# Key layer of a two-block transformer: ten chunks of the first table loaded while the queries are formed, and 100 tokens instead of 96 handled by gathered rows

## The chip, the core and the metric

The kernel runs on one core of a Trainium2 chip. The core has five engines that work side by side: TensorE (PE) multiplies matrices and writes to PSUM, VectorE (DVE) and ScalarE (ACT) do elementwise work, GpSimd (POOL) here issues the indirect loads, and SyncE (SP) issues most of the ordinary loads. Sixteen DMA engines move the data. The metric is the time of one execution on the device in microseconds (us). The median of three runs of the kernel before is 1599.38 us (1598.18 to 1601.05).

## What is computed

Two transformer blocks, one after the other, on 256 tokens of width 1024. The change lies in the last stage of the second block, the key layer:

```python
def peer(h, wq, keys1, keys2, u_tab, v_tab):      # per chunk of 128 tokens, xc: 128 x 1024
    q = (xc @ wq).reshape(128, 8, 2, 128)
    s1 = einsum('chd,hnd->chn', q[:, :, 0], keys1);  v1, i1 = top_k(s1, 16)
    s2 = einsum('chd,hnd->chn', q[:, :, 1], keys2);  v2, i2 = top_k(s2, 16)
    # the 16 best of the 256 sums, for each of 8 heads; expert = i1 * 128 + i2
    best, pos = top_k(v1[..., :, None] + v2[..., None, :] ..., 16)
    g = softmax(best)
    a = einsum('chkd,cd->chk', u_tab[eidx], xc)
    return einsum('chk,chkd->cd', gelu(a) * g, v_tab[eidx])
```

There are 128 x 128 = 16384 experts, each with a row of 1024 numbers in the first table (`u_tab`) and one in the second (`v_tab`). Every token picks 8 x 16 = 128 of them.

## The kernel before

The key layer handles the tokens in two ways at once.

**Dense tokens.** For the last ND = 160 of the 256 tokens (their count is ND = 256 - NG) every expert is computed. The tables are cut into 128 chunks of 128 experts; a chunk of a table is one load of 512 KB. In the first pass, for each chunk c, eight matmuls (L1640) multiply the chunk of the first table by the 160 tokens, and ACT applies the GELU and puts the result into column c of `B` (128 x 128 x 160, the activations' matrix; `act`, L1601). From chunk C0 = 40 on, the routing weights are multiplied in, four tokens at a time (`gbuild`; its four matmuls are L1968). In the second pass, for each chunk, eight matmuls (L1648) multiply `B` by the chunk of the second table and add up in eight PSUM buffers. So there are 1024 matmuls in each pass, with 160 columns each.

**Gathered tokens.** For the first NG = 96 tokens only the picked rows are fetched. They come in NS = 3 sets of GN = 32 tokens; one indirect load (L1768, issued by POOL) fetches 128 rows of 8 KB, first and second table side by side. DVE multiplies and sums these rows up (L1796, L1782); 32 such loads make a set, whose sums come into the dense result by eight small matmuls (L1653). `gathers(n)` is called once per chunk and lets so many steps of `gathered` be written down that they make 9/20 of the chunks of the first pass and 7/20 of those of the second. Step j issues gather j+4 (the first issues five), and a gather waits for the last matmul of the chunk before (`pace_pe`).

**Order of the work.** Before the first pass stand the queries: for each m of 16, `col_tile` loads a tile of `wq`, ACT (L97) and DVE (L98) split it in two parts, PE multiplies (L132 to L138), and two matmuls (L1564) give the scores, which ACT copies into a part of `B` not yet used (L1565). DVE searches the best 16 (`routing`, L1835 to L1911), 128 tokens after the other 128; for the first half it ends in `picks`, where ACT issues the DMAs that lay out the picked numbers (`gi`) and weights (`gw`) for the gathers (L1753). Three transposes on PE (L1928) take over the results of each half; they wait for DVE (the cast of L1921). `expand` (L1730, L1734) copies the gathered tokens' inputs on POOL, transposes them on PE and leaves one tile `xd` for each set.

**Loads.** The chunks of the tables take turns in ten buffers (four `wA`, three `hi`, three `lo`), and SP issues the load of a chunk (L87) when PE is done with the chunk that had the buffer. A scheduler puts the instructions of each engine in a fixed order by a timeline of its own.

The functions that the change touches follow; the line numbers are those of the profile.

Of the kernel before, what the change touches and what calls it, by code (L numbers as in the profile page):

```python
# [19 lines left out]
D = 1024  # L20
# [24 lines left out]
class K:  # L45
# [21 lines left out]
    def wload(self, src, shape, eng=None):  # L67
        pools = self.wpools
        p, tag = pools[self.wi % len(pools)]
        self.wi += 1  # L70
        if p is None:

            v = tag[:, :math.prod(shape)]
            if len(shape) == 2:
                v = v.rearrange("p (a b) -> p a b", a=shape[0])
            (eng or self.nc.sync).dma_start(v, src)
            return v
        if self.wrap and self.wi == len(pools):
# [8 lines left out]
        (eng or self.nc.sync).dma_start(v, src)  # L87
        return v
# [1439 lines left out]
    C0 = 40  # L1528
    NS, GN = 3, 32
    GG = 128 // GN  # L1530
    GJ = 128 // GG
    NG = NS * GN
    ND = S - NG

# [8 lines left out]
    def peer(self):  # L1543
# [14 lines left out]
        rg = self.routing([Bf[:, 128 * ND - 8192 + 2048 * t:128 * ND - 6144 + 2048 * t] for t in range(2)], Sc)  # L1558
        late = None

# [10 lines left out]
        for m in range(16):  # L1571
# [34 lines left out]

        nj = self.NS * self.GJ

        def gathers(n):
# [41 lines left out]
        def summed(s, k):  # L1651

            nc.tensor.matmul(acc[k][:, s * self.GN:(s + 1) * self.GN], self.sums[s][:, k * 128:(k + 1) * 128], self.sel,  # L1653
                             start=False, stop=False)

# [66 lines left out]
    def expand(self, x32):  # L1722

        nc = self.nc
        n, G = self.GN, self.GG
        self.picked = False
        self.gx = [self.T(self.rt, [128, D], F32, "xd%d" % s) for s in range(self.NS)]
        for s in range(self.NS):
            w = self.T(self.gp, [128, 2 * D], F32, "g")[:, 0:D].rearrange("p (k g t) -> p k g t", k=8, g=G)
            nc.gpsimd.tensor_copy(w, x32[:, :, None, s * n:(s + 1) * n].to_broadcast([128, 8, G, n]))  # L1730
            for hf in range(2):
# [6 lines left out]
    def picks(self, e0, e1, w):  # L1738

        nc = self.nc  # L1740
        n, J = self.GN, self.GJ
        t = self.T(self.gp, [128, 2 * D], F32, "g")
        f, wc, idi = t[:, 0:128], t[:, 128:256], t[:, 256:384].bitcast(I32)
        self.gi = self.T(self.rt, [128, self.NS, J], I32, "gi")
        self.gw = self.T(self.rt, [128, self.NS, J], F32, "gw")
        self.ga = self.T(self.rt, [128, self.NS, J], F32, "ga")
# [3 lines left out]
        for s in range(self.NS):  # L1750
# [3 lines left out]
        self.sel = self.T(self.rt, [128, n], F32, "gsel")  # L1754
        nc.scalar.dma_start(self.sel, self.A["sel"])
        self.picked = True

    def gathered(self):

        nc, A = self.nc, self.A  # L1760
        stt = nc.vector.scalar_tensor_tensor
        J, n = self.GJ, self.NS * self.GJ
        buf, acc = {}, self.T(self.rt, [128, D], F32, "xa")

        def fetch(i):
            if i < n:
                buf[i] = self.xg[:, i % 5 - 3, :] if i % 5 > 2 else self.T(self.gp, [128, 2 * D], F32, "g")
                ins = nc.gpsimd.indirect_dma_start(  # L1768
                    out=buf[i], out_offset=None, in_=A["uv"],
                    in_offset=bass.IndirectOffsetOnAxis(ap=self.gi[:, i // J, i % J:i % J + 1], axis=0))  # L1770
                if self.pace_pe:
# [4 lines left out]
        def add(i):  # L1776
            nonlocal acc
            s, j = i // J, i % J
            t, a, w = buf.pop(i)[:, D:], self.ga[:, s, j:j + 1], self.gw[:, s, j:j + 1]
            nc.vector.tensor_tensor(w, w, a, op=OP.mult)  # L1780
# [12 lines left out]
        for i in range(n):  # L1793
            s, j = i // J, i % J
            t, a = buf[i][:, 0:D], self.ga[:, s, j:j + 1]
            stt(t, t, 1.0, self.gx[s], op0=OP.mult, op1=OP.mult, accum_out=a)  # L1796
# [243 lines left out]
def _prep(I):  # L2040
# [54 lines left out]
    for n in ("w_gate", "w_up", "w_down"):  # L2095
# [23 lines left out]
                                 P["v"].reshape(-1, D)], 1))  # L2119
    P["sel"] = np.tile(np.eye(K.GN, dtype=np.float32), (K.GG, 1))  # L2120
    P["fnorm"] = _f(I["final_norm_g_2"][None])
# [36 lines left out]
```

## Time and profile before

| | |
|---|---|
| median of three runs | 1599.38 us (1598.18 to 1601.05) |
| profiled execution, its time | 1600.43 us |
| its span, from the first to the last instruction | 1598.6 us |
| PE busy | 1521.2 us (95%) |
| DVE busy | 954.7 us (60%) |
| ACT busy | 496.1 us (31%) |
| POOL busy | 125.7 us (8%) |
| moved by DMA | 536.5 MB, on average 336 GB/s |
| first pass of the key layer (L1640) | 975.9 to 1299.5 us |
| second pass (L1648) | 1299.5 to 1584 us |

The profile takes one execution; its span lies 1.8 us below that execution's own time. A float32 matmul stands as two records of PE. Records of PE overlap, so their pitch (the time of a long row divided by its count) is what one costs, not the duration of one. PEclk is the TensorE clock that was granted: 1.00 is 2.4 GHz and 0.50 is 1.2 GHz.

### The profile page before, as it was taken

How to read it: one execution, taken by the hardware profiler on the slowest of the kernel's cores; microseconds unless marked ns; L12 is line 12 of the kernel's file. 1: busy time of each engine (PE TensorE's matmuls, PEld its weight loads, DVE VectorE, ACT ScalarE, POOL GpSimd, SP SyncE). 2: the span in 40 equal slices, each digit the busy share in tenths (PEclk: the TensorE clock that was granted, in tenths of full speed). 3: DMA queues.
4: the chain of work that ended last, by engine and by line, in shares of the span. 5: the costliest groups of instructions: out<-in, count | busy, mean ns of one | idle time of the engine just before them, and what ended most of it. 6: DMA issues, size and time to landing. Idle time of an engine off the chain costs nothing. (4 is left out here: it accounts for less than half of the span.)

```text
span 1598.6 us, 25730 instructions
## 1 busy us (share of the span) xinstructions
PE 1521.2 (95%) x9872; PEld 1197.3 (75%) x9872; DVE 954.7 (60%) x2117; ACT 496.1 (31%) x1222; POOL 125.7 (8%) x122
## 2 busy tenths in 40 slices
PE   7999899999999998979999899999999999999996
PEld 6987744453434433359679699999999999999996
DVE  5995623333543533178978899876777874434441
ACT  5444422233312212156443543124444410000001
POOL 0000000000000000000000000121211221111111
PEclk9999899999999999999999999999999999999998
DMA  9547879999999999965658646999999999999992
GB/s 372 179 142 292 290 299 399 416 398 419 418 407 415 418 418 334 408 244 161 202 193 279 210 146 227 352 415 413 414 414 403 386 398 414 413 411 411 412 409 72
DMA packets 135324, 536.53 MB, mean 336 GB/s; under 512 B 16179, under 2 KB 17180, under 8 KB 122780
## 3 DMA queue, kind: packets, MB, share of 16 engines
q1 hardware_dynamic: 117184, 426.07, 70.1%
q0 software_dynamic: 13824, 100.67, 15.3%
q10 hardware_dynamic: 4188, 8.09, 1.4%
q8 instruction: 79, 1.29, 0.3%
q14 instruction: 49, 0.40, 0.1%
HBM read 532.57 MB, written 2.10 MB: 334 GB/s over the span
## 5 line engine op out<-in xcount | busy, mean ns | idle before, releaser
L1032 PE MATMUL ps<-wB,XT 128*64 128x512 f32 x476 | 129.1, 609 | 4.7 <-PEq L925 4.6
L132 PE MATMUL ps<-xh,hi 128*128 128x256 f32 x416 | 123.0, 297 | 1.8 <-ACT hi L97 1.8
L1796 DVE SCALAR_TENSOR_TENSOR g<-g,xd 128x1024 f32<-128x1024 f32 x58 | 70.9, 1223 | 82.4 <-DMA g<-in_uv_dram,gi 82.4
L138 PE MATMUL ps<-xh,lo 128*128 128x256 f32 x416 | 117.5, 283 | 0.5 <-DVE lo L98 0.5
L1640 PE MATMUL ps<-x,wA 128*128 128x160 f32 x832 | 117.8, 300 | 0.0
L137 PE MATMUL ps<-xl,hi 128*128 128x256 f32 x416 | 117.4, 283 | 0.3 <-DVE xl L305 0.3
L1648 PE MATMUL ps<-B,wA 128*128 128x160 f32 x832 | 115.4, 299 | 0.0
L1640 PEld LDWEIGHTS ps<-x,wA 128*128 128x128 f32 x832 | 114.7, 191 | 0.0
L1648 PEld LDWEIGHTS ps<-B,wA 128*128 128x128 f32 x832 | 113.7, 190 | 0.0
L1797 ACT ACTIVATE ga<-ga 128x1 f32<-128x1 f32 x96 | 19.3, 201 | 286.0 <-DVE g L1796 172.5
L1068 DVE SCALAR_TENSOR_TENSOR eyl<-ps,slotw,eyh 64x512 fp32r<-64x512 f32 x64 | 47.7, 745 | 90.3 <-ACT eyh L1067 89.6
L1032 PEld LDWEIGHTS ps<-wB,XT 128*64 128x64 f32 x476 | 38.5, 139 | 78.7 <-issue 70.9
L97 ACT ACTIVATE hi<-wA 128x1024 fp32r<-128x1024 f32 x63 | 66.6, 1059 | 75.4 <-PE ps L137 37.4
L98 DVE TENSOR_TENSOR lo<-wA,hi 128x1024 fp32r<-128x1024 f32 x63 | 76.7, 1221 | 19.9 <-ACT hi L97 17.8
L1081 DVE TENSOR_TENSOR h<-h,ps 128x512 f32<-128x512 f32 x64 | 41.8, 680 | 78.4 <-PE ps L1079 78.4
L1640 PE MATMUL ps<-x,hi 128*128 128x160 f32 x624 | 88.2, 299 | 0.0
L1768 POOL DMA_INDIRECT g<-in_uv_dram,gi x58 | 64.7, 1116 | 293.7 <-PE ps L1648 110.9
L1648 PE MATMUL ps<-B,hi 128*128 128x160 f32 x608 | 86.6, 300 | 0.0
L1640 PE MATMUL ps<-x,lo 128*128 128x160 f32 x592 | 86.2, 304 | 0.0
L1640 PEld LDWEIGHTS ps<-x,hi 128*128 128x128 f32 x624 | 85.6, 190 | 0.0
L132 PEld LDWEIGHTS ps<-xh,hi 128*128 128x128 f32 x416 | 79.4, 191 | 8.0 <-issue 4.6
L1648 PE MATMUL ps<-B,lo 128*128 128x160 f32 x608 | 84.8, 299 | 0.0
(541 smaller groups left out, 3310.4 us busy)
## 6 DMA issues: line engine op xcount, KB each, us to landing
wB<-in_w_gate_dram SPq DMA_DIRECT2D x68, 512.0 KB
wB<-in_w_down_dram SPq DMA_DIRECT2D x59, 512.0 KB
wA<-in_ut_dram SPq DMA_DIRECT2D x52, 512.0 KB
wA<-in_v_dram SPq DMA_DIRECT2D x52, 512.0 KB
wA<-in_ws_dram SPq DMA_DIRECT2D x51, 512.0 KB
wB<-in_w_up_dram SPq DMA_DIRECT2D x51, 512.0 KB
hi<-in_ut_dram SPq DMA_DIRECT2D x39, 512.0 KB
lo<-in_v_dram SPq DMA_DIRECT2D x38, 512.0 KB
```

What stands on the lines that cost most here:

```text
L97: ins = self.nc.scalar.activation(hi, w, AF.Copy)
L98: self.last_split = self.nc.vector.tensor_tensor(lo, w, hi.bitcast(F32), op=OP.subtract)
L132: ins = mm(ps, ah, bh, start=first, stop=False)
L137: mm(ps, ah, bl, start=False, stop=False)
L138: mm(ps, al, bh, start=False, stop=last)
L1032: nc.tensor.matmul(p[64 * s:64 * s + 64, :], XT[:, k, :], w[s][:, a, :], start=k == 0, stop=k == 7)
L1068: nc.vector.scalar_tensor_tensor(y[1][r, s, :], p[r, :], w, y[0][r, s, :].bitcast(F32), op0=OP.mult, op1=OP.subtract)
L1081: nc.vector.tensor_tensor(hh, hh, p, op=OP.add)
L1640: self.pace_pe = nc.tensor.matmul(p, w[:, k, :], x32[:, k, N0:], start=k == 0, stop=k == 7)
L1648: self.pace_pe = nc.tensor.matmul(acc[k][:, N0:], w[:, k * 128:(k + 1) * 128], B[:, c, :], start=c == 0, stop=c == 127)
L1768: ins = nc.gpsimd.indirect_dma_start(out=buf[i], out_offset=None, in_=A["uv"], in_offset=bass.IndirectOffsetOnAxis(ap=self.gi[:, i // J, i ...
L1796: stt(t, t, 1.0, self.gx[s], op0=OP.mult, op1=OP.mult, accum_out=a)
```

## The change

- NG goes from 96 to 100 and ND from 160 to 156. The sets are now a list `SETS`: three of 32 tokens and one of 4 tokens. A load of the small set fetches for 4 tokens 32 rows each, so that it has 4 loads: 100 gathers in all. `expand` makes four tiles, `gathered` and `summed` go by the list.
- `picks` keeps `gi` and `gw` as one column for each gather. For the small set the layout goes by way of DRAM: the numbers are stored there (`pk`) and loaded back in the other shape.
- The pace of the gathers in the first pass is 1/2 instead of 9/20.
- Ten chunks of the first table (`early`, NP = 10) are loaded into columns of `B` that are not in use yet, one after each tile of `wq` from m = 3 on, behind that tile's load on SP's queue. The first pass reads chunks 0 to 9 there and takes the ten buffers from chunk 10 on.

```diff
-    NS, GN = 3, 32
-    GG = 128 // GN
-    GJ = 128 // GG
-    NG = NS * GN
+    SETS = [(0, 32), (32, 32), (64, 32), (96, 4)]
+    NS = len(SETS)
+    NG = sum(n for _, n in SETS)
+    NP = 10
     ND = S - NG
...
             late = (m, q, kt[:, m % 8, :])
+            if m > 2 and len(early) < self.NP:
+
+                i = len(early)
+                w = Bf[:, 1536 + 1024 * i:2560 + 1024 * i].rearrange("p (k e) -> p k e", k=8)
+                self.after(nc.sync.dma_start(w, A["ut"][i].rearrange("p (k e) -> p k e", k=8)), self.last_load)
+                early.append(w)
...
-            while self.gn < min(nj, (n - self.g0) * 9 // 20 if n < 128 else
-                                (128 - self.g0) * 9 // 20 + (n - 128) * 7 // 20):
+            while self.gn < min(nj, (n - self.g0) // 2 if n < 128 else
+                                (128 - self.g0) // 2 + (n - 128) * 7 // 20):
...
-            w = self.wload(A["ut"][c].rearrange("p (k e) -> p k e", k=8), [8, 128])
+            w = early[c] if c < self.NP else self.wload(A["ut"][c].rearrange("p (k e) -> p k e", k=8), [8, 128])
...
-        for s in range(self.NS):
-            for d, q in ((self.gi, idi), (self.gw, wc)):
-                for g in range(self.GG):
-                    nc.scalar.dma_start(d[g * n:(g + 1) * n, s, :], q[s * n:(s + 1) * n, g * J:(g + 1) * J])
+        mem = []
+        for d, q in ((self.gi, idi), (self.gw, wc)):
+            for o, n in self.SETS:
+                if n < 32:
+
+                    m = self.T(self.dp, [n, 128], d.dtype, "pk%d" % len(mem))
+                    mem.append((d[:, o:o + n], m, n))
+                    nc.scalar.dma_start(m, q[o:o + n, :])
+                    continue
+                for g in range(128 // n):
+                    nc.scalar.dma_start(d[g * n:(g + 1) * n, o:o + n], q[o:o + n, g * n:(g + 1) * n])
+        for d, m, n in mem:
+            nc.scalar.dma_start(d, m.rearrange("t (g j) -> g t j", j=n))
```

The lines move: L1640 of before is L1648 in the changed kernel, L1928 is L1947, L1921 is L1940, L1601 is L1609, L1753 is L1767, L1734 is L1742.

Three places show how the scheduler's order moves. On PE, at the start of the first pass, where the first half's transposes stand among the chunks. Before:

```order
L1640 MATMUL ps_9934<-x_1898_9024,lo_9932 128x160 x8
L1928 MATMUL ps_9977<-ident_83,x_1909_9072 128x128
L1640 MATMUL ps_9985<-x_1898_9024,lo_9983 128x160 x8
L1640 MATMUL ps_10017<-x_1898_9024,wA_10015 128x160 x8
L1640 MATMUL ps_10045<-x_1898_9024,wA_10043 128x160 x8
L1928 MATMUL ps_9977<-ident_83,x_1909_9072 128x128 x2
L1640 MATMUL ps_10072<-x_1898_9024,wA_10070 128x160 x8
```

The same place in the changed kernel:

```order
L1648 MATMUL ps_9941<-x_1898_9024,B_8958 128x156 x8
L1947 MATMUL ps_9992<-ident_83,x_1909_9072 128x128
L1648 MATMUL ps_9998<-x_1898_9024,B_8958 128x156 x3
L1947 MATMUL ps_9992<-ident_83,x_1909_9072 128x128 x2
L1648 MATMUL ps_9998<-x_1898_9024,B_8958 128x156 x5
L1648 MATMUL ps_10030<-x_1898_9024,wA_10028 128x156 x8
```

The first transpose stands behind nine chunks in both; the other two stood behind twelve chunks and stand now behind nine and three matmuls of the tenth. The second half's three stand behind 29 chunks in both.

On SP, the loads while the queries are formed (`wq` tiles, the second half of the keys, then the first table). Before:

```order
L87 DMA wA_9181<-in_wq_dram 128x1024
L87 DMA wA_9228<-in_wq_dram 128x1024
L87 DMA wA_9275<-in_wq_dram 128x1024
L87 DMA wA_9322<-in_keysT_dram 128x1024
L87 DMA wA_9324<-in_wq_dram 128x1024
L87 DMA wA_9371<-in_wq_dram 128x1024
```

The same place in the changed kernel:

```order
L87 DMA wA_9183<-in_wq_dram 128x1024
L1591 DMA B_8958<-in_ut_dram 128x1024 x3
L87 DMA wA_9231<-in_wq_dram 128x1024
L1591 DMA B_8958<-in_ut_dram 128x1024
L87 DMA wA_9279<-in_wq_dram 128x1024
L1591 DMA B_8958<-in_ut_dram 128x1024
L87 DMA wA_9327<-in_keysT_dram 128x1024
L87 DMA wA_9329<-in_wq_dram 128x1024
L1591 DMA B_8958<-in_ut_dram 128x1024
L87 DMA wA_9377<-in_wq_dram 128x1024
```

Three early chunks stand in a row behind the sixth tile of `wq`, and then one behind each of the next seven tiles.

On ACT, where the first chunks' results leave PSUM (the exponent of the first half's softmax, the pick DMAs, the GELUs). Before:

```order
L1601 ACTIVATE B_8958<-ps_9752 128x160
L1601 ACTIVATE B_8958<-ps_9785 128x160
L1915 ACT_TABLE_LOAD
L1915 ACTIVATE x_1909_9072<-x_1909_9072 128x128
L1601 ACT_TABLE_LOAD
L1601 ACTIVATE B_8958<-ps_9817 128x160
L1753 DMA gw_9946<-g_9944 32x32 x2
```

The same place in the changed kernel:

```order
L1934 ACTIVATE x_1909_9072<-x_1909_9072 128x128
L1767 DMA gw_9953<-g_9951 32x32
L1609 ACT_TABLE_LOAD
L1609 ACTIVATE B_8958<-ps_9775 128x156
L1767 DMA gw_9953<-g_9951 32x32 x3
L1609 ACTIVATE B_8958<-ps_9806 128x156
```

The first two chunks' GELUs stood ahead of the exponent and stand now behind it, among the DMAs of `gw`.

## Rows read from the trace of the kernel before

**Rows 1.** Page: span; a DMA queue (packets, MB, share); issues of one form.

```profile
span 1598.6 us, 25730 instructions
...
q0 software_dynamic: 13824, 100.67, 15.3%
...
wA<-in_ut_dram SPq DMA_DIRECT2D x52, 512.0 KB
```

**Rows 2.** Busy time by stretch: us, engines, then PEclk, DMA share, GB/s.

```profile
990.00:995.00 5.00, 5.00 (x39) 5.00 (x38) 4.97 (x10) 0.91 (x3) 0.00 (x0) 1.00 0.39 99
...
1050.00:1100.00 50.00, 50.00 (x372) 50.00 (x371) 32.82 (x64) 19.97 (x76) 9.97 (x10) 0.98 1.02 415
1100.00:1150.00 50.00, 50.00 (x384) 50.00 (x383) 35.09 (x77) 24.39 (x96) 9.92 (x9) 1.00 1.02 413
1150.00:1200.00 50.00, 50.00 (x383) 50.00 (x382) 37.14 (x80) 23.61 (x97) 9.23 (x9) 1.00 1.02 414
...
1250.00:1300.00 50.00, 50.00 (x382) 50.00 (x381) 37.41 (x72) 18.82 (x85) 10.32 (x9) 1.00 0.99 394
```

**Rows 3.** Chain that ended last: start, us, what.

```profile
1078.10 0.89 PE ps L1968 x8
...
1319.41 1.70 PE ps L1653 x16
...
1398.96 178.57 PE ps L1648 x1314
```

**Rows 4.** The second pass's line, one of three forms: ns min/median/max, first and last start.

```profile
L1648 PE MATMUL ps<-B,hi x608: 299/299/383, 1312.7 to 1583.9; 128*128 128x160 f32 x152
```

**Rows 5.** PE in order of time; in brackets the idle time before, and its releaser.

```profile
912.64 3.73 PE L279 MATMUL ps<-ident,xxr 128*128 128x128 f32 x16 [5.25 <-DVE xxr L266]
...
975.00 1.09 PE L1734 MATMUL ps<-ident,g 128*128 128x128 f32 x8 [0.36 <-POOL g L1730]
...
996.91 0.30 PE L1928 MATMUL ps<-ident,x 128*128 128x128 f32 x1 [1.25 <-DVE x L1921]
...
1004.54 0.44 PE L1928 MATMUL ps<-ident,x 128*128 128x128 f32 x2 [0.75 <-DVE x L1921]
...
1045.69 0.69 PE L1928 MATMUL ps<-ident,x 128*128 128x128 f32 x2 [3.65 <-DVE x L1921]
```

**Rows 6.** Short stretches after two of these waits, columns as in rows 2.

```profile
917.00:922.00 5.00, 4.16 (x20) 4.16 (x21) 4.67 (x8) 3.26 (x8) 0.00 (x0) 0.52 0.24 91
1046.00:1048.00 2.00, 2.00 (x9) 2.00 (x8) 1.70 (x4) 0.84 (x4) 1.27 (x2) 0.50 1.03 414
```

**Rows 7.** DVE in order of time: the casts that the transposes wait for.

```profile
1004.26 0.23 DVE L1921 CAST x<-x 128x128 f32<-128x128 bf16 x1
...
1045.42 0.22 DVE L1921 CAST x<-x 128x128 f32<-128x128 bf16 x1
```

**Rows 8.** POOL in order of time; then the gathers' group and their time to landing.

```profile
973.90 1.04 POOL L1730 COPY g<-x 128x1024 f32<-128x1024 f32 x1 [48.26 <-PE ps L1734]
1011.99 1.25 POOL L1768 DMA_INDIRECT g<-in_uv_dram,gi  x1 [37.05 <-PE ps L1640]
```

```profile
L1768 POOL DMA_INDIRECT g<-in_uv_dram,gi x58: 939/939/1957, 1012.0 to 1547.1; - x58
...
DMA to landing us min/median/max: 8.4/8.9/10.5
```

**Rows 9.** ACT in order of time: the first pick DMAs.

```profile
989.06 1.25 ACTq L1753 DMA_DIRECT2D gw<-g  x2
```

**Rows 10.** SP in order of time; then one of its waits (total us, times, longest).

```profile
1012.61 3.60 SPq L87 DMA_DIRECT2D hi<-in_ut_dram  x3
...
1557.73 2.50 SPq L87 DMA_DIRECT2D hi<-in_v_dram  x2
```

```profile
SPq L87 <- PE ps L1640: 167.4, 78, 6.9
```

**Rows 11.** DMA from 1054 to 1084 us, where gathers and loads both have work queued.

```profile
DMA packets 2301, 12.47 MB, mean 416 GB/s; under 512 B 257, under 2 KB 257, under 8 KB 1306
```

**Rows 12.** A stretch of the queries, columns as in rows 2.

```profile
935.00:945.00 10.00, 10.00 (x89) 10.00 (x88) 10.00 (x50) 4.82 (x9) 0.00 (x0) 1.00 0.52 160
```

More of the change, by code (lines that the diff above doesn't have):

```diff
@@ L86, in wload @@
             v = v.rearrange("p (a b) -> p a b", a=shape[0])
-        (eng or self.nc.sync).dma_start(v, src)
+        self.last_load = (eng or self.nc.sync).dma_start(v, src)
         return v
@@ L1558, in peer @@
         rg = self.routing([Bf[:, 128 * ND - 8192 + 2048 * t:128 * ND - 6144 + 2048 * t] for t in range(2)], Sc)
-        late = None
+        late, early = None, []
         def score(m, q, kt):
@@ L1605, in act @@
                 tt(B[:, c, :tau], B[:, c, :tau], g[:, :tau], op=OP.mult)
-        nj = self.NS * self.GJ
+        nj = self.NG
         def gathers(n):
@@ L1651, in summed @@
         def summed(s, k):
-            nc.tensor.matmul(acc[k][:, s * self.GN:(s + 1) * self.GN], self.sums[s][:, k * 128:(k + 1) * 128], self.sel,
-                             start=False, stop=False)
+            o, n = self.SETS[s]
+            nc.tensor.matmul(acc[k][:, o:o + n], self.sums[s][:, k * 128:(k + 1) * 128], self.sel[n], start=False, stop=False)
         ns, ready = 0, []
@@ L1724, in expand @@
         nc = self.nc
-        n, G = self.GN, self.GG
         self.picked = False
         self.gx = [self.T(self.rt, [128, D], F32, "xd%d" % s) for s in range(self.NS)]
-        for s in range(self.NS):
+        for s, (o, n) in enumerate(self.SETS):
+            G = 128 // n
             w = self.T(self.gp, [128, 2 * D], F32, "g")[:, 0:D].rearrange("p (k g t) -> p k g t", k=8, g=G)
-            nc.gpsimd.tensor_copy(w, x32[:, :, None, s * n:(s + 1) * n].to_broadcast([128, 8, G, n]))
+            nc.gpsimd.tensor_copy(w, x32[:, :, None, o:o + n].to_broadcast([128, 8, G, n]))
             for hf in range(2):
@@ L1749, in picks @@
         nc.vector.tensor_copy(wc, w)
-        for s in range(self.NS):
-            for d, q in ((self.gi, idi), (self.gw, wc)):
-                for g in range(self.GG):
-                    nc.scalar.dma_start(d[g * n:(g + 1) * n, s, :], q[s * n:(s + 1) * n, g * J:(g + 1) * J])
-        self.sel = self.T(self.rt, [128, n], F32, "gsel")
-        nc.scalar.dma_start(self.sel, self.A["sel"])
+        mem = []
[10 more added lines that the diff above has]
+            nc.scalar.dma_start(d, m.rearrange("t (g j) -> g t j", j=n))
+        self.sel = {}
+        for n in sorted(set(n for _, n in self.SETS)):
+            self.sel[n] = self.T(self.rt, [128, n], F32, "gsel%d" % n)
+            nc.scalar.dma_start(self.sel[n], self.A["sel%d" % n])
         self.picked = True
@@ L1761, in gathered @@
         stt = nc.vector.scalar_tensor_tensor
-        J, n = self.GJ, self.NS * self.GJ
+        n = self.NG
+        where = [(s, j, J) for s, (_, J) in enumerate(self.SETS) for j in range(J)]
         buf, acc = {}, self.T(self.rt, [128, D], F32, "xa")
@@ L1777, in add @@
             nonlocal acc
-            s, j = i // J, i % J
-            t, a, w = buf.pop(i)[:, D:], self.ga[:, s, j:j + 1], self.gw[:, s, j:j + 1]
+            s, j, J = where[i]
+            t, a, w = buf.pop(i)[:, D:], self.ga[:, i:i + 1], self.gw[:, i:i + 1]
             nc.vector.tensor_tensor(w, w, a, op=OP.mult)
@@ L1793, in gathered @@
         for i in range(n):
-            s, j = i // J, i % J
-            t, a = buf[i][:, 0:D], self.ga[:, s, j:j + 1]
+            s = where[i][0]
+            t, a = buf[i][:, 0:D], self.ga[:, i:i + 1]
             stt(t, t, 1.0, self.gx[s], op0=OP.mult, op1=OP.mult, accum_out=a)
@@ L2119, in _prep @@
                                  P["v"].reshape(-1, D)], 1))
-    P["sel"] = np.tile(np.eye(K.GN, dtype=np.float32), (K.GG, 1))
+    for n in set(n for _, n in K.SETS):
+        P["sel%d" % n] = np.tile(np.eye(n, dtype=np.float32), (128 // n, 1))
     P["fnorm"] = _f(I["final_norm_g_2"][None])
```

9 lines of the change are left out of this document (4 added, 5 removed).

## The prediction

> **What bounds the kernel now.** The stretch to read is the key layer, from 976 us to the end. I read the chain that ended last first: from 1045.69 us on it is PE alone, chunk after chunk [rows 3, 5], and the second pass's last matmul starts at 1583.9 [rows 4], so PE ends at 1584.2. Then the stretches of 50 us: PE is busy without a gap, but the DMA engines are full as well, at 415, 413 and 414 GB/s from 1050 to 1200, and have a little to spare only later (394 GB/s) [rows 2]. So two resources stand at their limit at once, and what a change frees on the one it can take from the other. Then the waits of PE: four small ones, one for POOL at 975 and three for DVE's routing at 996.91, 1004.54 and 1045.69 [rows 5]. After the last of these the clock stands at 0.50, which is 1.2 GHz [rows 6].
>
> **PE, the columns.** A record of 160 columns costs 178.57 us / 1314 = 135.9 ns, one of 128 columns 0.89 / 8 = 111 ns, one of 32 columns 1.70 / 16 = 106 ns [rows 3]. Between 128 and 160 a column is worth 0.77 ns; in strict proportion 0.85. Four columns less give 3.1 to 3.4 ns on each of 4096 records (two records for each of 2048 matmuls): 12.7 to 13.9 us. I take 13.3; a chunk of 16 records goes from 2.174 to 2.122 us.
>
> **PE, the rest.** Eight transposes more in `expand`: about +0.9 us (975.00 to 975.93 for the last eight now). They wait for a fourth copy of POOL: 1.04 us, behind the third that starts at 973.90 [rows 8], so it is done at about 976.0 and costs PE another 0.2. Eight small matmuls for the fourth set: +1.7 [rows 3]; one `gbuild` step fewer (39 for 40): -0.9. Together with the columns -11.4 us.
>
> **The transposes moved up.** The two transposes that stood behind twelve chunks stand now behind nine and three matmuls, and they still need DVE's cast, which starts at 1004.26 [rows 7] at the end of a search that nothing here makes shorter. PE starts chunk 0 at about 977.1, has done nine at 996.2, waits to 996.9 as now, and three matmuls later, at 997.8, has nothing until 1004.5: 6.7 us idle where it was 0.75, so +5.9, and -0.5 for the first wait. An idle time of 5.25 us was followed by half the clock up to about 921.8 (0.52 on average from 917 to 922; 9.1 us of work), one of 3.65 us by half the clock up to about 1051.5 (0.98 on average from 1050 to 1100; 5.8 us) [rows 2, 5, 6]. So the new one costs another 2.9 to 4.5 us; I take 3.5. The third wait goes: PE comes to its place (29 chunks) after 1050, when the cast of 1045.42 [rows 7] is done: -3.65 and -2.9 of clock. Sum of the waits and the clock: about +2.3. If PE alone set the end, the change would bring -11.4 + 2.3 = **-9 us**.
>
> **The early chunks.** What they cost is hidden: while the queries are formed the DMA engines move 160 GB/s [rows 12], and 5.24 MB more over the 30 us make that some 335. What they bring is hidden as well. SP issues a load when PE is done with the chunk ten before it [rows 10], so chunk 20 waits for chunk 10 in both kernels, and from there on the loads can be ten chunks ahead and no more. The traffic that is taken away lies between 959 and 1012 us, where the engines have room anyway (99 GB/s at 990) [rows 2]. It gives nothing to the stretch behind 1014 us, in which they are full.
>
> **DMA.** There the change asks for more. A gather is 100.67 MB / 96 = 1.049 MB, a load 512 KB = 0.524 MB [rows 1]. Test on the kernel before: the first gather is issued at 1012 and its data flow from about 1014, when 24 loads have been asked for (the row at 1012.61 holds the 25th to 27th) [rows 10]; the last is issued at 1547.1 and lands 8.9 us later, at 1556 [rows 8], with about 250 of 256 loads landed (the row at 1557.73 holds the last two [rows 10]). That is 100.7 + 226 x 0.524 + 1.05 (the input read back between the passes) = 220.2 MB; at 414 GB/s, the mean of the three full stretches [rows 2], 531.9 us of the 542 there are. The kernel before has 10 us of DMA to spare, no more.
>
> The changed kernel: PE stands behind for the wait above. From 1004.5 it has half its clock for some 7 us and ends chunk 10 at about 1011.5, so at 1014 only 20 loads have landed. By its pace the last gather is issued behind chunk 233 (59 steps in the first pass, 37 more in 106 chunks of the second; the same count gives chunk 239 for the kernel before, which is 1546, and the row says 1547.1). It lands some 10 us later, when PE is at 238.7 and, with the loads just ahead of their use, 240 have landed: 104.9 + 1.05 + 220 x 0.524 = 221.3 MB, at 414 GB/s 534.5 us, up to 1548.5. The 17.3 chunks left take 36.7 us, the third and fourth set's sums 3.4: PE ends at 1588.6, against 1584.2 **+4.4 us**. This is later than PE alone would be (1575), so PE waits for loads on the way; its clock may fall for it, but as long as DMA sets the pace that costs nothing. The price of the rate: at 416 [rows 11] it is +1.8, at 413 +5.7, at 420, above any stretch of 50 us here, -3.2.
>
> The Trainium skill ("DMA: Bandwidth & Descriptors", Specifications) gives 435 GB/s as the ceiling of the way into SBUF and 358 as the memory's share for a core. The rows say neither: full stretches stand at 413 to 415. By the first figure, as an estimate, the 221.3 MB would take 509 us, and PE alone would set the end.
>
> **Costed at nothing.** The first chunks' GELUs move behind the exponent and the first pick DMA on ACT (989.06 [rows 9]): with a table load the first ends at about 991.3. PSUM has eight buffers, so the ninth chunk is the first to need one back, at 994: hidden by 2.7 us, and without that cover a stall of as much, ahead of a wait for DVE that swallows it. The DMAs by way of DRAM serve only the fourth set, whose first gather is the 97th. Four gathers more give DVE 4 x 2.7 us spread over 240 chunks; it has over 12 of every 50 us free [rows 2].
>
> **Rivals.** (1) *PE sets the end*: DMA keeps up, because gathers and loads interleave better than in the rows. -9 us: 1590.4. For it: PE never waits for a load now. Against it: it takes the 221.3 MB in some 521 us, 425 GB/s, and no stretch of 50 us has more than 415 there. This is faster than before. (2) *DMA sets the end, but PE isn't held at the transposes* (DVE comes earlier, or PE later): four more loads are asked for ahead of the gathers, -2.1 MB or -5 us: 1599. For it: the waits at 996.91 and 1004.54 were short ones, so the scheduler had DVE right there. Against it: PE's own work ahead of them can't fill 6.7 us. (3) *The early loads do harm*: they stand on SP's queue ahead of tiles of `wq`, each 0.524 MB or 1.26 us of the full rate. If half of the ten hold up a tile and through it DVE's search, which sets the gathers' start, that is +6 on the forecast: 1610. Against it: SP has 3.2 us between two tiles and the engines are half empty [rows 12]. (4) *The first chunks gain a real lead*, as the change says: it would show as a lead that lasts past chunk 20, and the buffers forbid that; it would take the time to that of rival 1.
>
> **How the numbers follow.** The profiled execution took 1600.43 us, 1.8 us beside its span of 1598.6 [rows 1], and the median is 1.05 below it. So +4.4 on the median of 1599.4: 1603.8. A measurement of this kernel can tell about 0.2%, 3.2 us, from no change. The forecast, DMA-bound with PE held, has a chance of 0.48; it spans 1600.5 to 1606 by its rates and is a slowdown in five cases of six (0.40), else no change (0.08). Rival 2: 0.25, no change but for its lower end (0.03 faster). Rivals 1 and 4: 0.19, faster. Rival 3: 0.08, slower. Faster 0.22, same 0.30, slower 0.48. The range leaves out rival 1's core and the tail of rival 3: 1592 to 1609.
>
> **What would show it.** PE idle for 6 to 7 us ahead of the two transposes and a clock of 0.50 after it; records of 156 columns at a pitch of 132.5 to 132.8 ns; the DMA engines at 413 to 416 GB/s in every stretch from 1050 to 1540, without the dip to 394; waits of PE for loads of the first table from about chunk 30 on; the last gather near 1540. If PE runs without waits from 1050 on and the GB/s rise above 420, rival 1 is right; if it doesn't wait at the transposes, rival 2; if the first gather starts later than 1014, rival 3.

## The result, and the profile after

The changed kernel takes 1613.1 us (1607.79 to 1614.3), the kernel before beside it 1599.28 (1598.18 to 1601.05): a ratio of 1.0076, between 1.0062 and 1.0090, or some 12 us slower. The forecast was 1603.8. The profiled execution took 1613.1 us, with a span of 1611.0.

The wait that was forecast is there. PE in order of time, around the first half's transposes:

```profile
998.63 0.30 PE L1947 MATMUL ps<-ident,x 128*128 128x128 f32 x1 [0.95 <-DVE x L1940]
998.77 1.02 PE L1648 MATMUL ps<-x,B 128*128 128x156 f32 x6
1006.27 0.69 PE L1947 MATMUL ps<-ident,x 128*128 128x128 f32 x2 [6.48 <-DVE x L1940]
```

PE stands idle for 6.48 us where it was 0.75 [rows 5]. Stretches of the same trace (us, engines, PEclk, DMA share, GB/s; columns as in rows 2):

```profile
1005.00:1010.00 5.00, 3.73 (x15) 3.73 (x16) 4.63 (x37) 0.30 (x1) 0.00 (x0) 0.50 0.02 3
...
1050.00:1100.00 50.00, 42.50 (x313) 40.94 (x312) 29.52 (x52) 15.55 (x60) 11.43 (x10) 1.00 1.02 415
1100.00:1150.00 50.00, 50.00 (x391) 50.00 (x390) 37.07 (x82) 25.44 (x100) 10.99 (x10) 1.00 1.02 413
1150.00:1200.00 50.00, 50.00 (x391) 50.00 (x390) 38.64 (x80) 23.72 (x96) 11.01 (x10) 1.00 1.02 415
...
1250.00:1300.00 50.00, 50.00 (x390) 50.00 (x389) 40.20 (x79) 20.28 (x89) 10.88 (x9) 1.00 1.02 412
1300.00:1350.00 50.00, 42.37 (x314) 40.96 (x313) 38.01 (x61) 3.98 (x19) 14.18 (x12) 1.00 1.02 415
1350.00:1400.00 50.00, 50.00 (x381) 49.97 (x380) 21.32 (x32) 1.62 (x8) 8.19 (x8) 1.00 1.02 414
```

The DMA engines are full in all of them; the dip to 394 [rows 2] is gone. PE is not: it stands idle for 7.5 us between 1050 and 1100 (6.5 of them for loads), where waits for loads were forecast, and for 7.6 us between 1300 and 1350, which the forecast doesn't name. PE there, in order of time:

```profile
1332.67 2.39 PE L1656 MATMUL ps<-B,lo 128*128 128x156 f32 x16 [1.37 <-DMA lo<-in_v_dram]
1336.43 2.39 PE L1656 MATMUL ps<-B,wA 128*128 128x156 f32 x16 [1.37 <-DMA wA<-in_v_dram]
1340.19 2.39 PE L1656 MATMUL ps<-B,wA 128*128 128x156 f32 x16 [1.37 <-DMA wA<-in_v_dram]
```

A chunk comes every 3.76 us, which is 0.524 MB / 3.76 us = 139 GB/s, a third of what the DMA engines move. Nearly all of the rest goes to gathers. POOL in order of time:

```profile
1309.56 1.18 POOL L1787 DMA_INDIRECT xm<-in_uv_dram,gi  x1 [3.34 <-PE ps L1656]
1312.45 1.18 POOL L1787 DMA_INDIRECT xm<-in_uv_dram,gi  x1 [1.71 <-DVE xd L1801]
1315.34 1.19 POOL L1787 DMA_INDIRECT g<-in_uv_dram,gi  x1 [1.71 <-DVE xd L1801]
1318.24 1.18 POOL L1787 DMA_INDIRECT g<-in_uv_dram,gi  x1 [1.71 <-PE ps L1656]
...
1330.99 0.94 POOL L1787 DMA_INDIRECT g<-in_uv_dram,gi  x1 [2.84 <-DVE xd L1801]
```

Six of them stand 2.9 us apart, where the pace of 7/20 asks for one in 6.1. They catch up: by the new pace 63 should have been issued when the first pass ends at 1305.0, and 57 were, as many as in the runs below with the old pace of 9/20 (b, c). From 1100 to 1300 more than half of POOL's waiting is for DVE; the largest share (us in all, times, longest):

```profile
POOL g L1787 <- DVE B L1613: 52.8, 12, 8.3
```

The start of the key layer differs from one execution to the next (chunk 0 begins between 971 and 981 us in the profiles here, whichever the kernel), so I compare profiles by stretch. The table gives us between the first records of chunks on PE; chunks 128 to 255 are the second pass, "queries" is from the first score matmul to chunk 0, "end" the end of the span. Each row is one execution.

| kernel | queries | 0 to 44 | 44 to 128 | 128 to 144 | 144 to 238 | 238 to end | from chunk 0 |
|---|---|---|---|---|---|---|---|
| before | 49.8 | 108.1 | 215.6 | 36.6 | 206.1 | 56.3 | 622.7 |
| changed | 54.7 | 115.4 | 211.1 | 44.9 | 203.5 | 57.6 | 632.6 |
| a, no early loads | 51.5 | 115.8 | 211.1 | 44.0 | 204.3 | 57.6 | 632.8 |
| b, even pace | 51.7 | 118.0 | 211.1 | 35.7 | 213.5 | 57.7 | 636.0 |
| c, old pace | 52.5 | 118.4 | 211.1 | 35.7 | 201.1 | 63.5 | 629.8 |
| d, transposes held | 51.7 | 114.4 | 211.1 | 44.5 | 204.2 | 57.6 | 631.7 |
| e, 96 tokens, early loads | 50.6 | 107.9 | 217.1 | 36.6 | 206.1 | 56.3 | 623.9 |
| f, before, transposes held | 50.8 | 110.7 | 216.7 | 36.6 | 206.1 | 56.3 | 626.4 |
| g, c and held | 52.4 | 114.8 | 211.1 | 35.7 | 201.1 | 62.1 | 624.8 |
| h, fewer loads | 52.0 | 111.7 | 211.7 | 35.7 | 212.5 | 57.6 | 629.2 |
| i, g and pace by stretch | 52.2 | 108.0 | 211.1 | 40.0 | 209.9 | 59.9 | 629.0 |
| j, f and pace by stretch | 49.8 | 101.4 | 215.6 | 39.6 | 206.1 | 57.3 | 620.1 |
| k, changed and pace by stretch | 51.9 | 107.6 | 211.1 | 39.6 | 209.7 | 60.0 | 628.0 |
| l, early loads 10 to 18 | 52.5 | 113.4 | 211.1 | 41.4 | 202.2 | 57.7 | 625.9 |
| m, g and early loads 10 to 18 | 50.7 | 107.7 | 211.1 | 35.7 | 201.1 | 63.8 | 619.5 |
| n, f and early loads 10 to 18 | 49.8 | 108.4 | 215.6 | 36.6 | 206.1 | 56.3 | 622.9 |
| o, m and held later | 54.7 | 102.3 | 214.0 | 35.7 | 201.1 | 60.5 | 613.6 |

Before to changed: +7.3, -4.5, +8.4, -2.5 and +1.3 from chunk 0 on, +9.9 together; chunk 0 itself begins 2.5 us later (978.4 for 975.9), with 4.9 us more in the queries. In the gbuild stretch (44 to 128) PE never waits and gains its columns; the losses stand to both sides of it.

### The profile page after: what moved, and what is told of

It reads as the page before. It is cut to its first block, busy times and chain, and to the rows that moved or that the text cites. A ratio compares the mean times of both kernels' runs of the same rounds, so it can differ in the third digit from the quotient of the medians.

```text
span 1611.0 us, 25775 instructions
## 1 busy us (share of the span) xinstructions
PE 1514.4 (94%) x9888; PEld 1185.8 (74%) x9888; DVE 968.6 (60%) x2131; ACT 494.4 (31%) x1220; POOL 131.6 (8%) x127
## 4 chain that ended last, share of the span: by engine, by line
PE 36%; DMA 16%; DVE 7%; ACT 1%; issue 1%; POOL 0%; ACTq 0%; POOLq 0%; SPq 0%; DVEq 0%
PE ps L1648 12%; PE ps L1656 8%; DMA wA<-in_v_dram 5%; DMA hi<-in_v_dram 3%; PE ps L137 2%; PE ps L132 2%; PE ps L138 2%; PE ps L1987 2%; DMA wA<-in_ut_dram 2%; PE ps L1032 1%; DMA lo<-in_ut_dram 1%; DVE lo L98 1%; DMA lo<-in_v_dram 1%; DMA hi<-in_ut_dram 1%; PE ps L1489 1%
## 5 line engine op out<-in xcount | busy, mean ns | idle before, releaser
L1656 PE MATMUL ps<-B,wA 128*128 128x156 f32 x832 | 114.1, 297 | 6.5 <-DMA wA<-in_v_dram 6.4
L1815 DVE SCALAR_TENSOR_TENSOR g<-g,xd 128x1024 f32<-128x1024 f32 x60 | 73.3, 1222 | 72.1 <-DMA g<-in_uv_dram,gi 71.9
L1648 PE MATMUL ps<-x,wA 128*128 128x156 f32 x768 | 107.1, 298 | 2.6 <-DMA wA<-in_ut_dram 1.6
L1648 PEld LDWEIGHTS ps<-x,wA 128*128 128x128 f32 x768 | 103.9, 192 | 3.3 <-ACT qp L1612 1.6
L1656 PE MATMUL ps<-B,hi 128*128 128x156 f32 x608 | 85.5, 297 | 0.3 <-DMA hi<-in_v_dram 0.3
L1656 PE MATMUL ps<-B,lo 128*128 128x156 f32 x608 | 83.3, 297 | 2.1 <-DMA lo<-in_v_dram 2.1
L1656 PEld LDWEIGHTS ps<-B,lo 128*128 128x128 f32 x608 | 81.4, 190 | 2.6 <-DMA lo<-in_v_dram 2.6
L1656 PEld LDWEIGHTS ps<-B,hi 128*128 128x128 f32 x608 | 81.8, 190 | 0.6 <-DMA hi<-in_v_dram 0.6
L137 PEld LDWEIGHTS ps<-xl,hi 128*128 128x128 f32 x416 | 79.4, 191 | 3.9 <-issue 3.1
```

What stands on the lines that cost most here:

```text
L137: mm(ps, ah, bl, start=False, stop=False)
L1648: self.pace_pe = nc.tensor.matmul(p, w[:, k, :], x32[:, k, N0:], start=k == 0, stop=k == 7)
L1656: self.pace_pe = nc.tensor.matmul(acc[k][:, N0:], w[:, k * 128:(k + 1) * 128], B[:, c, :], start=c == 0, stop=c == 127)
```

## The experiments

All ratios are to the kernel before, which was run beside each experiment (its median lay between 1598.7 and 1600.2 us), with their intervals; the letters are those of the table. In the expectations, "bytes" is the theory that the bytes which DMA has to move set the time.

**a. Without the early loads.** Do they do anything?

```diff
-    NP = 10
+    NP = 0
```

> The changed kernel without the ten early loads (the first table's chunks all go through the ten buffers again); 100 tokens, pace 1/2 and the order of PE stay. In the changed kernel's trace the load of chunk 20 is issued at 1012.6 us, behind chunk 10, with the early loads as it would be without. Theory 'bytes' (the DMA engines must have moved 223 MB between the first gather and the last one's landing, and early loads take nothing from that): no change but for the start, 1611 to 1613 us. Theory 'early loads delay the tiles of wq' (in the changed kernel the eleventh tile's load was issued some 1 us late, PE stood still and ran at half its clock from 946.3 to 949.7, and the first chunk began 2.5 us later): chunk 0 begins at 976 to 977 instead of 978.4 and the time is 1610.5 to 1611. Theory 'the early loads give a lead': without them slower, 1618 or more.

Measured: 1609.7 us, 1.0068 (1.0051 to 1.0086). The intervals of a and of the changed kernel overlap, and counted from chunk 0 the two profiles agree within 0.6 us at every place of the table. The early loads give no lead. The time lies 0.8 us below the nearest of the expected ranges, and the first two theories, half a microsecond apart, can't be told apart by it. Chunk 0 began at 972.8, but it began at 973.0 in b, with early loads, too: the late start isn't shown to be theirs.

**b. The same gathers, evenly.** Is the burst at the start of the second pass what costs?

```diff
-            while self.gn < min(nj, (n - self.g0) // 2 if n < 128 else
-                                (128 - self.g0) // 2 + (n - 128) * 7 // 20):
+            while self.gn < min(nj, (n - self.g0) * 9 // 20 if n < 128 else
+                                (128 - self.g0) * 9 // 20 + (n - 128) * 13 // 32):
```

> The changed kernel with the gathers' pace 9/20 in the first pass and 13/32 in the second, so that the last of the 100 gathers stands behind the same chunk 233 as in the changed kernel, but without the ten gathers at a pitch of 2.9 us at the start of the second pass (1309.6 to 1331.0). Theory 'bytes': the DMA engines are full either way and have the same bytes to move up to the last gather's landing; PE's waits for loads move from chunks 8 to 16 of the second pass to others, the time stays, 1611 to 1614 us. Theory 'burst' (the ten gathers in a row take two thirds of the DMA engines, and PE loses some 8 us there that it would otherwise not lose): 1604 to 1606.

Measured: 1614.6 us, 1.0099 (1.0082 to 1.0116). The burst is gone, and so are the waits there, but they come back as small ones up to the last gather:

```profile
1300.00:1350.00 50.00, 50.00 (x382) 50.00 (x381) 29.70 (x47) 2.72 (x13) 12.92 (x9) 1.00 1.02 415
...
1400.00:1450.00 50.00, 47.70 (x352) 46.52 (x351) 25.01 (x37) 1.83 (x9) 10.20 (x9) 1.00 1.02 414
1450.00:1500.00 50.00, 47.38 (x348) 45.97 (x346) 23.24 (x37) 1.82 (x9) 11.47 (x9) 1.00 1.02 413
1500.00:1550.00 50.00, 47.62 (x349) 46.49 (x350) 22.88 (x36) 1.83 (x9) 8.49 (x8) 1.00 1.02 414
```

The burst is only the form in which the bytes of the second pass show. "Bytes" stands, "burst" falls. The first stretch is 2.6 us longer than in the changed kernel, and 3.0 in c, with more waiting for loads, though no more gathers are issued in it (17 up to chunk 40 in all three); why stays open.

**c. The old pace.** 9/20 as in b, and 7/20 in the second pass, so that the last gather moves from behind chunk 233 to behind chunk 250.

> The changed kernel with the old pace of 9/20 in the first pass, 7/20 in the second as before: the last of the 100 gathers stands behind chunk 250 instead of 233. Theory 'bytes': each chunk that the last gather moves back lets 2.12 us pass for 1.27 us of load, 0.85 us of gain each, at most some 14 us; but the last gather then lands some 9 us later, at chunk 255, and the fourth set's sums wait for it and for two steps of DVE, 4 to 6 us at the end. Together 1603 to 1606, with PE idle ahead of the fourth set's small matmuls. Theory 'burst' alone (the pace matters only by the ten gathers in a row): -8 for the burst, +4 to 6 for the end, 1609 to 1611.

Measured: 1606.5 us, 1.0044 (1.0029 to 1.0059), at the upper end of what "bytes" has. PE is busy without a gap from 1100 to 1550, and the price at the end is there, in a row of PE's waits (us in all, times, longest):

```profile
PE ps L1662 <- DVE xd L1801: 2.3, 1, 2.3
```

**d. The transposes where they were**, behind twelve chunks:

```diff
+            if c == 11:
+                for t in self.tr[1:]:
+                    self.after(t, self.pace_pe)
```

> The changed kernel with the second and third transpose of the first half held behind twelve chunks, where they stood before the change; nothing else is edited (the scheduler puts two of the second half's behind 30.9 chunks instead of 29). PE no longer stands idle for 6.5 us behind nine chunks, nor runs at half its clock from 1000.9 to 1011.2. Theory 'bytes': PE is at chunk 14 instead of 11.6 when the first gather starts, four more loads have landed, 2.1 MB or 5 us: 1608 us, and PE waits for loads for some 12 us instead of 16.5. Theory 'PE's waits add up' (the transposes cost PE 10 us, and all of them come back): 1603. Theory 'the wait is hidden behind DMA altogether': 1613.

Measured: 1607.7 us, 1.0060 (1.0038 to 1.0082). The wait of 6.48 us is gone (PE's three waits there are 4.3 us in all), chunk 20 is reached 6 us earlier, and at chunk 44 one of these is left (114.4 for 115.4): PE waits for loads instead, 10.2 us in the first pass where it was 6.5. The time is the 1608 of "bytes", but its interval overlaps the changed kernel's, so no gain is shown by it.

**e. The early loads alone**: the changed kernel with three sets and 9/20.

> The ten early loads alone: the changed kernel with 96 tokens in three sets and the pace of 9/20, so that only the early loads (and the flat layout of gi, gw and ga) tell it from the kernel before. Theory 'bytes', with 'the early loads bring nothing': the load of chunk 20 is issued behind chunk 10 as before, the transposes stand where they stood, and the time is that of the kernel before, within 1.5 us. Theory 'they give a lead': 3 us or more faster. Theory 'they delay the tiles of wq': 2 to 3 us slower.

Measured: 1601.9 us, 1.0008 (0.9999 to 1.0017). No lead, no harm that can be measured. With a, the early loads are settled: the +12 comes with the 100 tokens, their pace and the order that the scheduler makes of them (with 96 tokens, as here, the two transposes still stand behind twelve chunks).

**f. The kernel before, freed of a wait.** The same three lines as in d with `c == 30`, for the second half's transposes. If 10 us of DMA were to spare, PE's 6.5 us must come back.

> The kernel before with one edit: the second half's last two transposes are held behind 31 chunks instead of 29. In the kernel before PE stands idle for 3.65 us ahead of them (1045.69) and then runs at half its clock for some 5.8 us, 2.9 us of which is lost. Theory 'at 96 tokens PE sets the end, with some 10 us of DMA to spare': all of it comes back, 6.5 us, 1592 to 1593. Theory 'DMA sets the end there too': no change, since the DMA engines are full from 1015 to 1200 either way and PE would only come to wait for loads instead, 1598 to 1599.

Measured: 1599.6 us, 0.9999 (0.9989 to 1.0008). Nothing came back. The wait of 3.65 us [rows 5] is gone, and in its place stand waits for loads, which the kernel before had none of:

```profile
1050.00:1100.00 50.00, 43.46 (x315) 41.89 (x314) 32.14 (x63) 19.13 (x74) 10.08 (x9) 1.00 1.02 416
1100.00:1150.00 50.00, 50.00 (x383) 50.00 (x383) 35.05 (x77) 24.93 (x99) 9.90 (x9) 1.00 1.02 413
1150.00:1200.00 50.00, 50.00 (x383) 50.00 (x383) 37.07 (x79) 23.53 (x96) 9.21 (x9) 1.00 1.01 405
1200.00:1250.00 50.00, 50.00 (x384) 50.00 (x383) 38.23 (x77) 23.27 (x97) 10.41 (x9) 1.00 1.00 385
```

PE stands idle for 6.5 us around 1075, 5.3 of them for loads, and at 1225 DMA moves 385 GB/s with room for more. What is to spare there can't be used 150 us earlier, nor later: the loads can be ten chunks ahead and no more. So the first stretch, from the first gather to about chunk 44, has a balance of its own.

**g. c with both halves' transposes held**, behind 12 and 31 chunks.

> The changed kernel with the pace of 9/20 and both halves' transposes held, behind 12 and behind 31 chunks: 100 tokens and the early loads remain. PE's own work and waits are now some 9 us below the kernel before. Theory 'bytes': of these only what lets more loads land ahead of the gathers counts, four chunks or 5 us below the run with the pace alone (1606.5): 1601 to 1602, with more waits for loads between chunks 25 and 47. Theory 'PE's waits add up': 1590 to 1592.

Measured: 1602.2 us, 1.0002 (0.9988 to 1.0016): "bytes", and 10 us above "PE's waits add up". Against c the first stretch gains 3.6 us, so with the old pace holding the transposes brings more than the 1 us of d. Waits for DVE ahead of the transposes (6.6 us) and for loads (5.3 us) are left, all of them ahead of 1100.

**h. Fewer bytes, same PE.**

```diff
+            if c % 16 < 15:
                 w = self.wload(A["v"][c], [1024])
```

(and the same for the first table's loads)

> The changed kernel with every sixteenth load of either table left out from chunk 15 on (16 loads, 8.4 MB; the chunk before is multiplied once more in its place, so part of the computation is changed); all matmuls, gathers and their order stay. It takes bytes away and nothing from PE. Theory 'bytes': 14 of these loads lie ahead of the last gather's landing, 7.3 MB or 17.8 us of DMA; PE's waits for loads, 16.5 us in the changed kernel, go except for those around chunk 40, which two or three loads fewer shorten by 3: 1599 to 1603. Theory 'the waits for loads come from the order of the queue, not from the bytes' (the burst at the start of the second pass, and the start): they stay, 1609 to 1613.

Measured: 1606.7 us, 1.0045 (1.0031 to 1.0059). Half of what "bytes" expected: 5 us by the ratios, for 10 to 14. The gain stops where the lead is full:

```profile
1200.00:1250.00 50.00, 50.00 (x391) 50.00 (x390) 39.77 (x79) 23.38 (x97) 8.88 (x9) 1.00 0.99 385
1250.00:1300.00 50.00, 50.00 (x389) 50.00 (x388) 37.29 (x74) 18.98 (x84) 9.69 (x9) 1.00 0.99 388
1300.00:1350.00 50.00, 46.36 (x349) 45.65 (x348) 37.73 (x59) 3.04 (x15) 14.68 (x15) 1.00 1.02 416
1350.00:1400.00 50.00, 44.35 (x329) 43.17 (x329) 24.45 (x38) 1.82 (x9) 7.55 (x7) 1.00 1.02 414
```

What was saved up to 1300 is idle DMA at 385 GB/s, and the waits at the start of the second pass are as long as before. One sum over all bytes falls here, as in f; a sum for each stretch stands.

**i, j, k. Gathers moved out of the first stretch.** A pace of 1/4 up to chunk 40 and 1/2 behind it, on g (i), on f (j) and on the changed kernel (k); in the second pass 3/8, in j 7/20.

```diff
+            while self.gn < min(nj, (n - self.g0) // 4 if n < 40 else
+                                (40 - self.g0) // 4 + (min(n, 128) - 40) // 2 + max(n - 128, 0) * 3 // 8):
```

> The kernel before with its second half's transposes held behind 31 chunks, as in the run that brought nothing (1599.6), and with the pace 1/4 up to chunk 40, 1/2 up to the end of the first pass, then 7/20 as before. The waits for loads between chunks 37 and 47, 6.5 us, had taken the place of the transposes' wait there. Theory 'a balance for each stretch': with four gathers fewer in that stretch they go, and the 6.5 us come back at last: 1592 to 1594. Theory 'one balance over all bytes': the kernel before had bytes to spare as a whole, so moving gathers changes nothing, 1598 to 1600.

> The run with the pace of 9/20 and both halves' transposes held, with another pace: 1/4 up to chunk 40, 1/2 up to the end of the first pass, 3/8 in the second. 100 tokens and the early loads remain, the last gather stands behind chunk 247. The bytes are the same, but some four gathers, 4.2 MB, are moved out of the stretch from the first gather to chunk 44 into the stretch of gbuild, where the DMA engines dip below 413 GB/s because the loads can be only ten chunks ahead. Theory 'a balance for each stretch' (what the DMA engines can't use in gbuild's stretch is lost, and the first stretch has a balance of its own): the waits for loads there (5.3 us) and most of the wait at the end (1.6) go, and the waits for DVE ahead of the second half's transposes get shorter, since fewer gathers stand among DVE's search: 1592 to 1596. Theory 'one balance over all bytes': no gain from that, 1601 to 1604.

> The changed kernel with the pace 1/4 up to chunk 40, 1/2 up to the end of the first pass and 3/8 in the second, and nothing else. The transposes' wait behind nine chunks, 6.5 us and the half clock after it, stays. Theory 'a balance for each stretch': the waits for loads around chunk 40 (7.5 us) go, and those of the second pass (9 us) as well, since the last gather stands behind chunk 247 instead of 233: 1597 to 1600, some 7 us below the run with the pace of 9/20 alone (1606.5). Theory 'one balance over all bytes': as that run, 1603 to 1606.

Measured: j 1594.6 us, 0.9969 (0.9958 to 0.9980); i 1606.5, 1.0042 (1.0029 to 1.0055); k 1608.2, 1.0043 (1.0031 to 1.0055). In all three the first stretch does what its own balance says: 101.4 for 110.7 (j), 108.0 for 114.8 (i), 107.6 for 115.4 (k). In j that is the gain: faster than both kernels. In i and k the time lies above the ranges of both theories. In i the second pass takes the gain back (249.9 for 236.8 in g); k is some 5 us faster than the changed kernel, but the waits of its second pass, 9.7 us for 8.9, stay, and it is no faster than c. I had expected gbuild's stretch to take up the gathers that were moved (11 are issued up to chunk 40 in i, 17 in g). It doesn't: from chunk 40 to 128 40 gathers are issued in both, 0.45 for a chunk, at the pace 1/2, which asks for 44, as at 9/20. DVE lets no more through: 59.2 of the 110 us from 1130 to 1240 in i are waits of POOL for the end of DVE's step on `B` (L1613). They go into the second pass, whose balance is used up with 100 tokens:

```profile
1200.00:1250.00 50.00, 50.00 (x391) 50.00 (x390) 40.09 (x81) 22.85 (x98) 12.92 (x10) 1.00 1.01 400
...
1500.00:1550.00 50.00, 47.27 (x349) 46.10 (x349) 21.44 (x32) 1.62 (x8) 9.22 (x8) 1.00 1.02 413
```

**l, m, n. Early loads that count.** If the gate is the number of loads landed at the first gather, the early chunks must be those that come behind the ten buffers' first filling.

```diff
-    NP = 10
+    NP = 9
...
-                w = Bf[:, 1536 + 1024 * i:2560 + 1024 * i].rearrange("p (k e) -> p k e", k=8)
+                w = Bf[:, 2560 + 1024 * i:3584 + 1024 * i].rearrange("p (k e) -> p k e", k=8)
...
-            w = early[c] if c < self.NP else self.wload(A["ut"][c].rearrange("p (k e) -> p k e", k=8), [8, 128])
+            w = early[c - 10] if 10 <= c < 10 + self.NP else self.wload(A["ut"][c].rearrange("p (k e) -> p k e", k=8), [8, 128])
```

(the loads take `A["ut"][10 + i]`)

> The changed kernel with its early loads fetching chunks 10 to 18 instead of 0 to 9 (nine of them, in columns of B that are overwritten later), nothing else by hand. The ten buffers then hold chunks 0 to 9, come free from 980 us on, while the DMA engines are half empty, and the loads can be nineteen chunks ahead: 29 have landed at the first gather instead of 20, 4.7 MB or 11 us of DMA. Theory 'a balance for each stretch': the waits for loads around chunk 40 (7.5 us) go, those at the start of the second pass (9 us) stay, since the lead is down to ten buffers by then: 1604 to 1607; up to 4 us of it may come back as a longer wait for DVE ahead of the second half's transposes. Theory 'one balance over all bytes': 11 us, 1601 to 1603. Theory 'the gathers' share of the queue starves the loads whatever has landed': no change, 1611 to 1614.

> The same early loads of chunks 10 to 18 in the run with the pace of 9/20 and the transposes held (1602.2), whose waits for loads, 5.3 us, all lie around chunk 40. 100 tokens. Theory 'a balance for each stretch': these go, 1596 to 1599; with PE earlier, DVE's search may hold it longer ahead of the second half's transposes, which stand behind 34.6 chunks now. Theory 'the gathers' share': no change, 1601 to 1603.

> The same early loads of chunks 10 to 18 with 96 tokens, the pace of 9/20 and the second half's transposes held (the scheduler puts them behind 33.1 chunks): the run f_hold96 with early loads that raise the number of loads landed at the first gather from 24 to 29. Theory 'a balance for each stretch': the 6.5 us of waits for loads that had taken the place of the transposes' wait go, 1592 to 1594, as the slower pace ahead of chunk 40 did (1594.6). Theory 'the gathers' share': no change, 1599 to 1600.

Measured: l 1604.0 us, 1.0024 (1.0012 to 1.0037); m 1596.2, 0.9976 (0.9964 to 0.9989); n 1600.0, 1.0005 (0.9995 to 1.0014). l and m came out as "a balance for each stretch" has it. In none of the three does PE wait for a load in the first pass any more, so the cause of those waits is settled: the loads that have landed ahead of the gathers. What follows differs: n gained nothing. By its time alone it would be "the gathers' share"; its trace, without waits for loads, says otherwise. PE now waits for DVE ahead of the second half's transposes (in l, in m, in n):

```profile
1058.74 0.69 PE L1947 MATMUL ps<-ident,x 128*128 128x128 f32 x2 [4.94 <-DVE x L1940]
```

```profile
1057.51 0.69 PE L1951 MATMUL ps<-ident,x 128*128 128x128 f32 x2 [5.47 <-DVE x L1943]
```

```profile
1052.48 0.69 PE L1951 MATMUL ps<-ident,x 128*128 128x128 f32 x2 [3.56 <-DVE x L1943]
```

It is DVE that has become later. The cast that they wait for, in n and then in f, without the early loads:

```profile
1052.20 0.23 DVE L1943 CAST x<-x 128x128 f32<-128x128 bf16 x1
```

```profile
1043.14 0.22 DVE L1924 CAST x<-x 128x128 f32<-128x128 bf16 x1
```

That is 79.9 us behind chunk 0 in n and 71.9 in f. Between the two halves' transposes DVE has 19 multiplications and sums of gathered rows to do in n (10 and 9) and 10 in f (6 and 4), at 1.2 to 1.3 us each: the gathers' work stands ahead of the search's end in DVE's order. So n exchanged waits for loads for a wait on DVE.

**o. m with its wait taken away**: the second half's transposes held behind 37 chunks, and written down four chunks later.

```diff
+            for _ in range(4 * t):
+                yield
             p = self.ps()
```

> The run with 100 tokens, early loads of chunks 10 to 18, the pace of 9/20 and the transposes held (1596.2), with the second half's last two transposes held behind 37 chunks instead of 34.6 (and written down four chunks later, so that they take a later PSUM buffer). There PE stood idle for 5.5 us ahead of them, up to 1057.5, and ran at half its clock behind that. Theory 'a balance for each stretch, and DVE's search is the next to hold PE': 5.5 us and some 2.9 us of clock come back, less what gbuild has to wait at chunk 40: 1588 to 1591. Theory 'DMA takes its place again': PE waits for loads between chunks 37 and 47 instead, where the lead was 6 to 10 us, 1594 to 1597.

Measured: 1592.8 us, 0.9962 (0.9948 to 0.9976), the fastest here. The first stretch is down from 107.7 to 102.3, but the next one is up from 211.1 to 214.0: PE still waits 1.93 us at the transposes, and for loads again, 1.7 us between 1097 and 1104, where I had expected none. So it came out between the two theories. In this run 100 tokens, with the old pace, the transposes held and a lead that lasts, are some 6 us faster than the kernel before; against the best with 96 tokens (j, 0.9969) the intervals overlap, so it isn't shown that 100 tokens pay more than 96.

## Why the prediction was wrong

- **Two resources at their limit, and DMA the later one: right.** PE did wait for loads, from chunk 36 on. No stretch of 50 us of the key layer moved more than 416 GB/s, and the time went up, so rivals 1 and 4 are out; PE was held at the transposes, so is rival 2.
- **Columns: right.** In the second pass PE's row without a wait, in the chain that ended last, gives 42.50 / 320 = 132.8 ns for a record (132.5 to 132.8 forecast), and the gbuild stretch is 4.5 us shorter, 84 chunks of 0.053 us.

```profile
1375.18 42.50 PE ps L1656 x320
```

- **The transposes: right**, 6.48 us for 6.7, at half the clock behind it. But d shows that the wait is worth no more than one microsecond at chunk 44 with the new pace, because waits for loads take its place; with the old pace it is 3.6 (g against c).
- **The early loads: right**, gated by the buffers of chunks 10 to 19. SP asks for chunk 20 at 1012.57 (about 1011.5 forecast), and in a, without early loads, at the same distance behind chunk 0 within 0.5 us:

```profile
1012.57 2.45 SPq L87 DMA_DIRECT2D wA<-in_ut_dram  x2
```

- **The queries: too low.** +1.1 us was forecast for the fourth set; the profile has +4.9, others with 100 tokens +0.9 to +4.9. A tile of `wq` came late there and ACT waited 4.15 us for it at 944.09. Rival 3 may have a small part in that; e and n, with early loads, have 50.6 and 49.8. It stays open.
- **The DMA sum: the step that failed**, in size and in form. The last gather's data end at 1554.4 us. DMA from 1014 to 1554, by queue (packets, MB, share):

```profile
DMA packets 46883, 222.64 MB, mean 412 GB/s; under 512 B 5444, under 2 KB 5448, under 8 KB 34036
## 3 DMA queue, kind: packets, MB, share of 16 engines
q1 hardware_dynamic: 32141, 117.11, 54.2%
q0 software_dynamic: 14399, 104.86, 47.2%
q8 instruction: 32, 0.52, 0.4%
q14 instruction: 15, 0.12, 0.1%
```

In size: (117.11 - 1.05) / 0.524 = 221.5 loads for 220, and 0.64 MB of instructions that I had left out, 222.64 MB for 221.3; at 412 GB/s, the start included, not 414. That is 3.2 and 2.6 us: landing at 1554.4 for 1548.5. The rest of the chunks and the sums take 1.8 us more than the 40.1 of the forecast, and the second pass's last matmul ends at 1596.3 for 1588.6, 12.1 us behind the kernel before where 4.4 were forecast. So of the 7.7 us that the forecast of PE's end lacks, 5.9 are the DMA sum. How much of them is due to the late start of chunk 0 isn't shown. A sum of some 535 us was asked to give a difference of 4, and it was off by 1.1%, which is more than that difference.

In form: "10 us of DMA to spare" in the kernel before was true of the sum and of no use. The spare lies from 1200 to 1300, behind a lead that ten buffers cap; the first stretch had none (f), and neither had the second pass once gathers were pushed into it (b, i, k). The forecast treated the two places where the change takes from DMA, four loads less at the first gather and a denser pace, as one.

- **The pace: wrong.** I took the new pace as kept. DVE doesn't keep it, and six gathers of the first pass come in the second. By b this cost nothing that can be measured in itself, but moving the last gather back (c) is worth 5 us.

## What to carry to other kernels

Where a lead is capped by buffers, make the balance of a shared resource for each stretch between the points where the lead is full or empty: what is spare in one can't pay for another, and a wait removed there can come back as the next one (for loads in f, for DVE in n). A load made early pays only if it opens the gate of the loads behind it: ten chunks ahead of the buffers changed nothing that could be measured, nine placed behind their first filling took away every wait for a load in the first pass (l, m, n), which paid with 100 tokens and not with 96. A difference of two large sums is no forecast unless each term is known better than the difference.

## What the runs showed of the hardware

How two queues share the DMA engines when both have work was not part of the forecast. From 1310 to 1340 us, in the changed kernel:

```profile
q0 software_dynamic: 1106, 8.14, 65.5%
q1 hardware_dynamic: 1180, 4.31, 35.9%
```

The gathers (q0) and the loads (q1) moved about the same number of packets, 1106 and 1180, and the gathers' are about twice as large, 8 KB rows against 4 KB. So in this stretch the loads get a third of the bandwidth. The same holds from 1066 to 1080 us (532 packets and 534) and in the kernel before from 1054 to 1084 (1120 and 1178). The Trainium skill ("DMA: Bandwidth & Descriptors", Queues, rings and completion order) says that each engine goes round the queue rows packet by packet, a packet there being several descriptors. These rows agree as far as the totals go, and show what comes of it when the rows of data are unequal; in which order single packets went isn't shown.
